# A two-layer encoder trunk on one core: splitting weights further ahead at the start of a feed-forward stage, and a later place for two small steps

## The chip, the cores and the metric

The kernel runs on one core of a Trainium2 chip. The metric is the device time of one execution in microseconds (us). The core has a matrix engine (TensorE, PE in the profile, with its weight loads as PEld), VectorE (DVE), ScalarE (ACT), GpSimd (POOL) and SyncE (SP, which only issues transfers here). Each engine works through its own instructions in order, and semaphores hold an instruction back until its inputs are there.

## The reference

The input x is 256 tokens by 1024, in float32. The network has two layers; each adds half of a gated feed-forward network, then attention of two kinds, then half of a second feed-forward network:

```python
def swiglu(h, w_gate, w_up, w_down):
    return (jax.nn.silu(h @ w_gate) * (h @ w_up)) @ w_down

for l in range(DEPTH):
    x = x + 0.5 * swiglu(rms_norm(x, ffn1_norm[l]), ffn1_w_gate[l], ffn1_w_up[l], ffn1_w_down[l])
    h = rms_norm(x, mix_norm[l])
    proj = h @ w_in[l]
    ...
    x = x + jnp.concatenate([out_a, out_b], axis=-1) @ w_out[l]
    x = x + 0.5 * swiglu(rms_norm(x, ffn2_norm[l]), ffn2_w_gate[l], ffn2_w_up[l], ffn2_w_down[l])
return rms_norm(x, final_norm)
```

The gate and up matrices are 1024 by 2816, the down matrix is 2816 by 1024. So a call runs four feed-forward stages, two per layer.

## The kernel before

**Split products.** TensorE multiplies in a rounded float32 format (`fp32r`). To keep precision every operand is split in two: the high part is the value cast to `fp32r` (by ScalarE), the low part is the value less the high part (by VectorE). A product is then three matmuls: high by high, low by high, high by low. Weights are loaded raw (tiles `raw`, of which there are 6), and split on the core into tiles `w` of the pool `s4` (28 tiles, for everything of that size).

**Steps and the planner.** All weights are listed at the start in the order of use, as steps of 1 MB (`specs`; a step is `Step`, one use of it `Split`). A step is split in two halves, each one cast and one subtraction of 128 x 1024 (`emit_split`, L191 to L217). `ahead(n)` (L228) places, at the point of the program where it is called, the splits of all halves up to number n, the preparations of the steps that need one, and the loads for which a raw tile is free. It is called from `weights` (L249), which hands out the next step i and works ahead up to half 2i + `look[0]` (less an argument), and from `Split.part` (L182), at the first use of the second half of step i, up to half 2i + 1 + `look[0]`; a step taken with `held=True` doesn't make this second call. The number `look[0]` is thus how many halves the splitting runs ahead of the use. All engines but SyncE keep the order in which the program issues their instructions (`Kept`), so where a split is placed decides what it stands behind on ScalarE and on VectorE. SyncE's loads are issued in the order in which they are placed, and each waits until its raw tile has been split.

**A feed-forward stage** (`ffn`, L600) goes through the 2816 columns in five groups of 512 and a rest of 256. Group 0 is plain: four steps (gate and up, for the first and the second half of the 1024 rows) go into the sums `gs` and `us`. While it runs, the norm of the stage is still being finished: the residual's last two turned pairs and the squares (`before(1)`), then the row statistics (`before(2)`, that is `Norm.stats`, L397: mean on VectorE, power -1/2 on GpSimd giving `r`, and half of it, `hr`, on VectorE). `r` is used in the gates (silu, scaled by `r`), `hr` in the up products (`up`, L612). At the end of `before(2)` the accumulating transfers held back till then are issued on GpSimd (`flush`).

**Groups 1 to 4 of a later stage** (`by_seven`, L632) use seven products in place of eight, in the manner of Strassen and Winograd. `SEVEN` names the groups: in the first stage of the call 2, 3 and 4, in the three later ones 1 to 4, so `1 in sevens` is true in these alone. This needs sums of operands:
- of the norm's output: `Norm.copies` (ScalarE) takes float32 copies, `make_sums` (L349) forms four differences on VectorE and splits them; the first two subtractions read only the copies.
- of the weights: raw tiles a, b, c and d. Half of the sums are formed by accumulating transfers on GpSimd (`gather`, L126: b into a, c into b), half by VectorE, which adds c and then d into a (`plus`, L131), two instructions each.

A group has nine steps: a, (b + c), d, c, the first down step, then a three times in its summed forms, and the second down step; in group 1 the order is a, d, down, c, (b + c) and so on. In a group the first product of the gate's upper left part is kept in `m1`, the second added to it on VectorE to give `g0` (for one half of the tokens), and a silu on ScalarE is applied to `g0` in place. `g0` is read only at the end of the group, in `up`.

**look[0]** is 8 in feed-forward stages (`IN_FFN`), but 7 in group 0 of a later one; in groups 1 to 4 of a later stage 8, 7, 6 and 5; 6 (`IN_MIX`) at its end and in attention.

Of the kernel before, what the change touches and what calls it, by code (L numbers as in the profile page):

```python
# [29 lines left out]
IN_FFN, IN_MIX = 8, 6  # L30
# [4 lines left out]
def trunk(ctx: ExitStack, tc: tile.TileContext, x, n1, g1, u1, d1, nm, w_in, sink,  # L35
# [44 lines left out]
    def tmp(tag="tmp", bufs=5, shape=(P, 2, 256), dt=F32):  # L80
        return tp.tile(list(shape), dt, tag=tag, bufs=bufs, name=nm_(tag))
# [143 lines left out]
    look = [IN_MIX]  # L225
# [23 lines left out]
    def weights(less=0, held=False):  # L249

        i = at["use"]
        at["use"] += 1
        if i > 1:
            ahead(2 * i + look[0] - less)
        w = loaded[i]
        w.held = held
        return w
# [48 lines left out]
    class Norm:  # L306
# [90 lines left out]
        def stats(self, n=512):  # L397
            ms = tmp("ms", 2, (P, 2))
            dve.tensor_reduce(ms, self.ss.rearrange("p t (h q) -> p t h q", q=n // 256)[:, :, :, 0],
                              axis=mybir.AxisListType.X, op=ALU.add)  # L400
            dve.tensor_scalar(ms, ms, 1.0 / D, EPS, op0=ALU.mult, op1=ALU.add)
            self.r = tmp("r", 2, (P, 2))
            pool.tensor_tensor(self.r, ms, mhalf[:, 0:2], op=ALU.pow)
            self.hr = tmp("hr", 2, (P, 2))
            dve.tensor_scalar_mul(self.hr, self.r, 0.5)

# [30 lines left out]
    norm = Norm(0)  # L437
# [162 lines left out]
    def ffn(norm, aside=None, before=None, final=False, sevens=SEVEN[1]):  # L600
        def silu(out_, acc, t):
            act.activation(out_, acc, AF.Silu, scale=norm.r[:, t:t + 1])
            return out_

        def gate(gs):
            g = []
            for t in range(2):
                n = gs[t].shape[1]
                g.append(silu(tmp().rearrange("p a n -> p (a n)")[:, :n], gs[t], t))
            return g  # L610

        def up(h, acc, g, t):  # L612
            n = acc.shape[1]
            dve.scalar_tensor_tensor(h[:, t, :n], in0=acc, scalar=norm.hr[:, t:t + 1], in1=g, op0=ALU.mult, op1=ALU.mult)

        def hidden(g, us):
            h = blk(F32)
            for t in range(2):
                up(h, us[t], g[t], t)
            return h  # L620

        def prod(xo, w):
            acc = bank()
            for k in range(4):
                hi, lo = w.part(k)
                xh, xl = xo(k)
                pe.matmul(acc, lhsT=xh, rhs=hi, start=k == 0, stop=False)
                pe.matmul(acc, lhsT=xl, rhs=hi, start=False, stop=False)
                pe.matmul(acc, lhsT=xh, rhs=lo, start=False, stop=k == 3)
            return acc  # L630

        def by_seven(h, g):  # L632


            flat = lambda: tmp().rearrange("p a n -> p (a n)")

            def put(o, x, y, op):
                dve.tensor_tensor(o, x, y, op=op)
                return o

            m1, m7 = flat(), flat()
            if g > 1:
                act.copy(m1, prod(norm.quarter(0, 0), weights()))
                act.copy(m7, prod(norm.summed(3), weights(held=True)))
                hT = turn(h, 2)
                p2 = prod(norm.quarter(0, 1), weights())
                g0 = put(flat(), p2, m1, ALU.add)
                p3 = prod(norm.summed(2), weights())
                silu(g0, g0, 0)
                down(hT, g - 1, 0, weights())  # L650
            else:
                p1 = prod(norm.quarter(0, 0), weights(1, True))
                hT = turn(h, (0,))
                w = weights(1, True)
                act.copy(m1, p1)
                p2 = prod(norm.quarter(0, 1), w)
                hT += turn(h, (1,))
                g0 = put(flat(), p2, m1, ALU.add)
                w = weights()
                silu(g0, g0, 0)  # L660
                down(hT, 0, 0, w)
                p3 = prod(norm.summed(2), weights())
                act.copy(m7, prod(norm.summed(3), weights()))
            h = blk(F32)
            p5 = prod(norm.summed(0), weights())
            late, run = g == max(sevens), 1 in sevens
            p6 = prod(norm.summed(1), weights(look[0] - 5 if late else run, late or run))
            u2 = put(flat(), p6, m1, ALU.subtract)
            u3 = put(m7, m7, u2, ALU.add)
            p4 = prod(norm.quarter(1, 1), weights(look[0] - 4 if late else 3 * run, late or run))  # L670
            g1 = put(m1, p4, u3, ALU.subtract)
            w = weights(look[0] - 3 if late else 2 * run)
            silu(g1, g1, 1)
            put(u3, u3, p5, ALU.subtract)
            put(u2, u2, p5, ALU.subtract)
            put(u2, u2, p3, ALU.add)
            up(h, u2, g0, 0)
            up(h, u3, g1, 1)
            down(hT, g - 1, 1, w)
            return h  # L680

        def turn(hs, n):
            out_ = []
            for i in (range(n) if isinstance(n, int) else n):
                sl = halves(bank())
                for c in range(2):
                    for t in range(2):
                        pe.transpose(sl[:, c, t * P:(t + 1) * P], hs[:, t, (2 * i + c) * P:(2 * i + c + 1) * P], ident)
                hb = blk()
                split(hb, sl)  # L690
                out_.append(hb)
            return out_

        accs = [[bank(), bank()] for _ in range(2)]

        def down(hT, g, h, w):
            tokens(accs[h], [None] * (2 * g) + hT, w, 4 * g, last=(FC - 1, G4 - 1) if final and h else FC - 1)


        gs, us = [bank(), bank()], [bank(), bank()]  # L700
        if before is None:
            before = norm.late
        look[0] = IN_FFN - (1 in sevens)
        before(0)
        ws = (weights(), weights(2))
        for k in (0, 2):
            if k:
                before(1)
            for sl, w in zip((gs, us), ws):
                tokens(sl, norm.xs, w, 0, (k, k + 1))  # L710
                if k and 1 in sevens:
                    norm.copies(2)
        before(2)
        look[0] = IN_FFN
        if 1 in sevens:
            sums = norm.make_sums()
            next(sums)
            w = weights()
            next(sums)
            next(sums)  # L720
            tokens(gs, norm.xs, w, 4)
            w = weights(0, True)
            g = gate(gs)
            next(sums)
        else:
            tokens(gs, norm.xs, weights(), 4)
            g = gate(gs)
            w = weights()
        tokens(us, norm.xs, w, 4)
        h = hidden(g, us)  # L730
        if 1 in sevens:
            next(sums)
        for n in range(1, NGRP):
            if n in sevens:
                look[0] = IN_FFN + min(sevens) - n if before is not take_x else IN_MIX - (n == NGRP - 1)
                h = by_seven(h, n)
                continue
            sums = norm.make_sums()
            gs = [bank(), bank()]
            tokens(gs, norm.xs, weights(), 0)  # L740
            hT = turn(h, 2)
            norm.copies()
            next(sums, None)
            tokens(gs, norm.xs, weights(), 4)
            g = gate(gs)
            next(sums, None)
            us = [bank(), bank()]
            for k0 in (0, 4):
                tokens(us, norm.xs, weights(), k0)
                next(sums, None)  # L750
            h = hidden(g, us)
            for hh in range(2):
                down(hT, n - 1, hh, weights())
                if hh == 0:
                    next(sums, None)

        gu = [bank(), bank()]
        tokens(gu, norm.xs, weights(), 0)
        hT = turn(h, 2)
        tokens(gu, norm.xs, weights(), 4)  # L760
        h = hidden(gate([b[:, 0:256] for b in gu]), [b[:, 256:512] for b in gu])

        def rest():
            hE = turn(h, 1)
            if aside is not None:
                aside()
            return hE
        return accs, hT, rest
# [294 lines left out]
    for l in range(DEPTH):  # L1063
# [7 lines left out]
        if not final:  # L1071
            norm = Norm((l + 1) * 8)
# [76 lines left out]
```

## Time and profile before

| | |
|---|---|
| time, median of 3 runs | 928.06 us (927.64 to 929.15) |
| the profiled execution, its own time | 928.21 us |
| its span | 926.4 us |
| mean granted clock of TensorE | 0.999 |
| ScalarE casts of weights, 128 x 1024 and smaller | 458, mean 952 ns |
| VectorE subtractions of weights | 458, mean 1102 ns |
| VectorE sums of raw tiles | 60, mean 1223 ns |
| HBM read | 199.00 MB, 216 GB/s over the span |

Nearly all instructions carry one line number, that of the helper that issues them (L50), so the profile is read by tiles: `w<-raw` is the cast of a weight half, `w<-raw,w` its subtraction, `raw<-raw,raw` a sum of raw tiles, `tmp<-tmp,r` the silu of a group's g0 or g1, `tmp<-ps,r` a gate of group 0, `ps` anything that TensorE writes. A row of a timeline has the start in us from the span's start, the duration in us (from the first to the last of a merged run), engine, line, operation, output and inputs, shapes, the count behind an x, and in brackets how long the engine had been idle before and what ended that. A row of the waits has engine and output, what it waited for, total us, times, and the longest.

### The profile page before, as it was taken

To read this page: it belongs to the slowest core of one execution; us is meant where nothing else is said; L and a number is where in the kernel's file an instruction comes from. 1 tells how busy PE (TensorE), PEld (TensorE's weight loads), DVE (VectorE), ACT (ScalarE), POOL (GpSimd) and SP (SyncE) were. 2 spreads that over 40 slices of the span, in tenths; PEclk is the share of its full clock that TensorE was granted. 3 is DMA by queue.
4 is the path that set the end of the run, shared out by engine and by line. 5 is a ranking of instruction groups with operands and counts; after the bars stand their busy time and mean duration, and the time that the engine had idled before them with its cause. 6 is when DMAs were issued, how large, how long until landed. Compare 5 with 4: busy or idle time off the path is not lost.

```text
span 926.4 us, 12577 instructions
## 1 busy us (share of the span) xinstructions
PE 909.5 (98%) x4696; PEld 763.2 (82%) x4696; DVE 807.0 (87%) x1125; ACT 590.1 (64%) x917; POOL 65.1 (7%) x83
## 2 busy tenths in 40 slices
PE   8999999999999999999999999999999999999997
PEld 6888887899888888877888887778998888888776
DVE  6769999869875999999779999997698679999994
ACT  7846676567755776576485675665578486675561
POOL 0401000000000100100010010000001010010011
PEclk9999999999999999999999999999999999999999
DMA  9997898837346598897776998787462476998831
GB/s 335 349 236 210 249 268 272 234 104 220 127 139 176 141 291 247 240 265 272 264 170 182 292 261 234 237 289 227 115 230 92 137 170 181 285 273 238 240 134 46
DMA packets 114061, 200.87 MB, mean 217 GB/s; under 512 B 3662, under 2 KB 31376, under 8 KB 114000
## 3 DMA queue, kind: packets, MB, share of 16 engines
q1 hardware_dynamic: 96528, 166.74, 53.6%
q0 software_dynamic: 16096, 31.75, 19.0%
q10 hardware_dynamic: 1376, 1.57, 0.5%
q8 instruction: 37, 0.61, 0.3%
q14 instruction: 24, 0.20, 0.1%
HBM read 199.00 MB, written 1.05 MB: 216 GB/s over the span
## 4 chain that ended last, share of the span: by engine, by line
PE 57%; DVE 26%; DMA 9%; issue 4%; ACT 3%; ACTq 0%; POOLq 0%; DVEq 0%; POOL 0%
PE ps L50 57%; DVE w L50 17%; DMA raw<-in_ffn_w_up_dram 9%; DVE raw L50 3%; DVE tmp L50 3%; ACT w L50 3%; DVE s L50 2%; DMA xk<-in_x_dram 0%; ACT tmp L50 0%; ACTq L50 0%; DVE xk L50 0%; DVEq L50 0%; DVE v L50 0%; POOLq L1144 0%; DVE q L50 0%
## 5 line engine op out<-in xcount | busy, mean ns | idle before, releaser
L50 PE MATMUL ps<-w,s 128*128 128x512 f32 (+1 forms) x2574 | 603.1, 391 | 3.1 <-DVE w L50 3.1
L50 PEld LDWEIGHTS ps<-w,s 128*128 128x128 f32 x2574 | 476.7, 188 | 105.0 <-DVE w L50 6.6
L50 DVE TENSOR_TENSOR w<-raw,w 128x1024 fp32r<-128x1024 f32 (+1 forms) x458 | 482.5, 1102 | 34.8 <-ACT w L50 34.1
L50 ACT CAST w<-raw 128x1024 fp32r<-128x1024 f32 (+1 forms) x458 | 410.8, 952 | 142.8 <-DVE raw L50 96.2
L50 PE MATMUL ps<-w,q 128*128 128x512 f32 x540 | 127.3, 389 | 0.0
L50 PEld LDWEIGHTS ps<-w,q 128*128 128x128 f32 x540 | 101.4, 188 | 21.0
L50 PE MATMUL ps<-s,w 128*128 128x256 f32 x672 | 84.0, 285 | 0.0
L50 PEld LDWEIGHTS ps<-s,w 128*128 128x128 f32 x672 | 81.7, 191 | 1.1
L50 POOL DMA_DIRECT2D raw<-in_ffn_w_up_dram x30 | 38.9, 1295 | 483.6 <-DVE w L50 164.8
L50 DVE TENSOR_TENSOR raw<-raw,raw 128x1024 f32<-128x1024 f32 x60 | 70.7, 1223 | 0.0
L50 ACT ACTIVATE s<-ps,gcol 128x256 fp32r<-128x256 f32 (+1 forms) x80 | 31.7, 480 | 46.9 <-PE ps L50 45.2
L50 PE MATMUL ps<-w,v 128*128 128x512 f32 x180 | 44.1, 391 | 2.9 <-DVE w L50 2.9
L50 PEld LDWEIGHTS ps<-w,v 128*128 128x128 f32 x180 | 33.6, 188 | 11.0 <-DVE w L50 4.2
L50 PE MATMUL ps<-ident,s 128*128 128x128 f32 x304 | 41.2, 274 | 0.2
L50 PEld LDWEIGHTS ps<-ident,s 128*128 128x128 f32 x304 | 35.1, 140 | 6.9 <-DVE s L50 1.2
L50 ACT CAST s<-ps 128x512 fp32r<-128x512 f32 x44 | 24.3, 595 | 23.5 <-PE ps L50 23.5
L50 ACT ACTIVATE s<-s,negm 128x256 f32<-128x256 f32 x64 | 31.9, 500 | 6.6 <-DVE negm L50 6.4
L50 DVE TENSOR_TENSOR tmp<-ps,tmp 128x512 f32<-128x512 f32 x49 | 33.7, 687 | 2.5 <-PE ps L50 1.6
L50 ACT COPY tmp<-ps 128x512 f32<-128x512 f32 x34 | 19.8, 583 | 23.0 <-PE ps L50 17.4
L50 DVE SCALAR_TENSOR_TENSOR s<-ps,gcol,s 128x256 fp32r<-128x256 f32 x48 | 20.3, 478 | 14.9 <-ACT s L50 14.8
L50 DVE TENSOR_TENSOR s<-ps,s 128x512 fp32r<-128x512 f32 x44 | 28.8, 687 | 4.0 <-ACT s L50 4.0
L50 ACT ACTIVATE tmp<-tmp,r 128x512 f32<-128x512 f32 x30 | 21.6, 721 | 15.2 <-DVE tmp L50 15.0
(106 smaller groups left out, 406.8 us busy)
## 6 DMA issues: line engine op xcount, KB each, us to landing
raw<-in_ffn_w_down_dram SPq DMA_DIRECT2D x44, 1024.0 KB, 8.5
raw<-in_ffn_w_gate_dram SPq DMA_DIRECT2D x39, 1024.0 KB, 5.3
raw<-in_ffn_w_up_dram SPq DMA_DIRECT2D x39, 1024.0 KB, 5.2
raw<-in_ffn_w_up_dram POOLq DMA_DIRECT2D x30, 1024.0 KB, 11.5
raw<-in_w_in_dram SPq DMA_DIRECT2D x14, 1024.0 KB, 5.3
raw<-in_ffn_w_gate_dram SPq DMA_DIRECT2D x8, 512.0 KB, 4.6
raw<-in_ffn_w_up_dram SPq DMA_DIRECT2D x8, 512.0 KB, 5.5
raw<-in_w_in_dram SPq DMA_DIRECT2D x8, 512.0 KB, 5.4
```

Of the source, the lines that this page charges most:

```text
L50: ins = issue(*a, **k)
```

## The change

It acts on the three later feed-forward stages (`run = 1 in sevens`), and, in the place of `hr`, on all norms.

1. `look[0]` in group 0: 8 in place of 7 up to the turned pairs, then 9 in place of 7 for the second half of the first two steps, and 9 in place of 8 until group 1, where it is 8 as before.
2. The halving of `r` leaves `stats` and becomes `halve`. It is called behind the sums' first two subtractions in the later stages, and directly behind the statistics in the first one; in the attention stages, which don't use `hr`, it isn't called.
3. The silu of `g0` in groups 1 to 4 of the later stages stands behind the first down product with its splits, not ahead of it.

```diff
@@ Norm.stats
             self.r = tmp("r", 2, (P, 2))
             pool.tensor_tensor(self.r, ms, mhalf[:, 0:2], op=ALU.pow)
+
+        def halve(self):
             self.hr = tmp("hr", 2, (P, 2))
             dve.tensor_scalar_mul(self.hr, self.r, 0.5)
@@ by_seven
+            late, run = g == max(sevens), 1 in sevens
             m1, m7 = flat(), flat()
             if g > 1:
...
                 p3 = prod(norm.summed(2), weights())
-                silu(g0, g0, 0)
+                if not run:
+                    silu(g0, g0, 0)
                 down(hT, g - 1, 0, weights())
+                if run:
+                    silu(g0, g0, 0)
             else:
...
                 g0 = put(flat(), p2, m1, ALU.add)
-                w = weights()
+                down(hT, 0, 0, weights())
                 silu(g0, g0, 0)
-                down(hT, 0, 0, w)
...
-            late, run = g == max(sevens), 1 in sevens
@@ ffn
-        look[0] = IN_FFN - (1 in sevens)
+        look[0] = IN_FFN
         before(0)
         ws = (weights(), weights(2))
         for k in (0, 2):
             if k:
                 before(1)
+                look[0] = IN_FFN + (1 in sevens)
...
         before(2)
-        look[0] = IN_FFN
         if 1 in sevens:
             sums = norm.make_sums()
             next(sums)
+            norm.halve()
             w = weights()
...
         else:
+            norm.halve()
             tokens(gs, norm.xs, weights(), 4)
```

## The prediction

> **What bounds the kernel now.** I read the page's busy shares first, then busy time by windows over one later stage (the feed-forward half that opens layer 1), then the timelines of TensorE, VectorE and ScalarE there.
>
> ```profile
> PE 909.5 (98%) x4696; PEld 763.2 (82%) x4696; DVE 807.0 (87%) x1125; ACT 590.1 (64%) x917; POOL 65.1 (7%) x83
> ...
> PE ps L50 <- DVE w L50: 6.0, 10, 1.0
> ...
> 488.00:607.00 119.00, 117.01 (x529) 95.82 (x528) 117.20 (x121) 75.15 (x87) 7.70 (x6) 1.00 0.84 240
> ```
>
> The windows row is start:end, length, then busy time of TensorE, its weight loads, VectorE, ScalarE and GpSimd. Averaged over the kernel TensorE rules; in the grouped part of a later stage TensorE (117.0 of 119.0) and VectorE (117.2) are level, and the waits row says who is late: in ten places a matmul waits for a low half that VectorE has just written. I take the stalls from starts, since a record (0.39 us) is longer than the pitch of a 512-wide matmul (24 records from 566.99 fill 5.44 us, 0.227 each).
>
> ```profile
> 490.49 0.89 PE L50 MATMUL ps<-ident,s 128*128 128x128 f32 x4
> ...
> 493.96 0.60 PE L50 MATMUL ps<-ident,s 128*128 128x128 f32 x4
> ...
> 566.99 5.61 PE L50 MATMUL ps<-w,q 128*128 128x512 f32 x24
> 572.43 0.63 PE L50 MATMUL ps<-w,s 128*128 128x512 f32 x2
> 573.50 1.67 PE L50 MATMUL ps<-w,s 128*128 128x512 f32 x6 [0.44 <-DVE w L50]
> ...
> 584.07 1.97 PE L50 MATMUL ps<-w,v 128*128 128x512 f32 x8
> 587.01 1.19 PE L50 MATMUL ps<-w,v 128*128 128x512 f32 x4 [0.96 <-DVE w L50]
> ...
> 605.24 0.65 PE L50 MATMUL ps<-w,s 128*128 128x512 f32 x2
> 606.42 1.88 PE L50 MATMUL ps<-w,s 128*128 128x512 f32 x7 [0.52 <-DVE w L50]
> ```
>
> Four losses: the turn at 490.49 takes 0.89 us where the next takes 0.60 (T0 = 0.3); two matmuls from 572.43 should be followed at 572.88 and are at 573.50 (S1 = 0.6); eight from 584.07 at 585.89, but at 587.01 (S2 = 1.1); two from 605.24 at 605.69, but at 606.42 (S3 = 0.7). Together 2.7 us; three later stages of one build hold about 8 us, and that is all the change can win, because nothing else makes TensorE wait there. VectorE runs through without a break from 488 on, so TensorE's end follows VectorE's. To win, VectorE must be ahead when the run begins, or lose its gaps within it.
>
> **Group 0: splits further ahead.** A split of half a step is a ScalarE cast (high half) and a VectorE subtraction (low half). By the planner's counters I number the halves from group 1's first step: h0, h1 (a), h2, h3 (d), h4, h5 (down), h6, h7 (c). Before, h0 comes at gs's second half, h1 and h2 at us's, h3 and h4 behind the sums' subtractions, h5 and h6 around the third step, h7 at group 1. After: h0 before the turned pairs, h1 and h2 at gs's second half, h3 and h4 at us's (before the statistics), h5 behind the subtractions, h6 and h7 with the third and fourth steps. Nothing is added; from group 1 on the order is as before. ScalarE and VectorE in that stretch:
>
> ```profile
> 471.19 1.57 ACT L50 ACTIVATE s<-ps,gcol 128x256 fp32r<-128x256 f32 x4 [3.31 <-PE ps L50]
> ...
> 474.02 1.03 ACT L50 CAST w<-raw 128x1024 fp32r<-128x1024 f32 x1
> 474.96 1.56 ACT L50 ACTIVATE s<-ps,gcol 128x256 f32<-128x256 f32 x4
> ...
> 481.81 1.35 ACT L50 CAST q<-tmp 128x512 fp32r<-128x512 f32 x2
> ...
> 484.96 1.25 ACT L50 ACTIVATE tmp<-ps,r 128x512 f32<-128x512 f32 x2
> ...
> 491.41 0.59 ACT L50 CAST s<-ps 128x512 fp32r<-128x512 f32 x1 [2.62 <-PE ps L50]
> 491.89 2.01 ACT L50 CAST w<-raw 128x1024 fp32r<-128x1024 f32 x2
> ```
> ```profile
> 472.06 1.66 DVE L50 SCALAR_TENSOR_TENSOR s<-ps,gcol,s 128x256 fp32r<-128x256 f32 x4 [1.36 <-ACT s L50]
> 475.09 1.23 DVE L50 TENSOR_TENSOR w<-raw,w 128x1024 fp32r<-128x1024 f32 x1 [1.37 <-ACT w L50]
> 477.49 2.36 DVE L50 TENSOR_TENSOR w<-raw,w 128x1024 fp32r<-128x1024 f32 x2 [1.17 <-ACT w L50]
> ...
> 481.01 0.17 DVE L50 TENSOR_SCALAR hr<-r 128x2 f32<-128x2 f32 x1 [0.89 <-POOL r L50]
> ...
> 489.37 1.41 DVE L50 SCALAR_TENSOR_TENSOR s<-ps,hr,tmp 128x512 f32<-128x512 f32 x2
> ...
> 493.02 0.69 DVE L50 TENSOR_TENSOR s<-ps,s 128x512 fp32r<-128x512 f32 x1
> 493.62 1.22 DVE L50 TENSOR_TENSOR w<-raw,w 128x1024 fp32r<-128x1024 f32 x1
> ```
>
> Prices: casts follow each other at 0.95, subtractions at 1.13, and a subtraction starts 1.07 behind its cast (474.02, 475.09). h0's cast fits into ScalarE's 3.31 us of waiting for TensorE (467.9 to 468.8); its subtraction fills VectorE's gap before 472.06. h1 and h2 are cast from 474.02, four copies follow (1.56), h3 and h4 are cast at 477.5 and 478.4, subtracted until 480.8; the second copies end at 481.0. The statistics come 1.05 us later than before, the sums' first subtraction at 481.1, as before, with two more halves behind it.
>
> **The norm's halving.** `hr` no longer stands ahead of the subtractions, which need only the copies.
>
> ```profile
> 480.27 0.71 POOL L50 TENSOR_TENSOR r<-ms,mhalf 128x2 f32<-128x2 f32 x1 [5.82 <-DVE ms L50]
> 480.95 1.33 POOL L50 DMA_DIRECT2D raw<-in_ffn_w_up_dram  x1
> ...
> 495.08 2.00 ACT L50 CAST w<-raw 128x1024 fp32r<-128x1024 f32 x2
> ...
> 497.09 2.36 DVE L50 TENSOR_TENSOR w<-raw,w 128x1024 fp32r<-128x1024 f32 x2
> ...
> 488.34 0.37 SPq L153 DMA_DIRECT2D raw<-in_ffn_w_gate_dram  x1
> ...
> raw<-in_ffn_w_gate_dram SPq DMA_DIRECT2D x39, 1024.0 KB, 5.3
> raw<-in_ffn_w_up_dram POOLq DMA_DIRECT2D x30, 1024.0 KB, 11.5
> ```
>
> The power ends near 482.0, while VectorE subtracts until 482.5, so the 0.89 us of waiting goes; the halving itself stays (0.1). Its price from both sides: 0.9 saved, or 0.2 if the power and the subtractions get in each other's way for its 0.71 us. Two of the six halvings, in the attention stages, fall away; the diagonals behind them need `r` anyway: nothing. Behind the power on GpSimd waits the transfer that accumulates b into a. It moves from 480.95 to 482.0 and lands, by its median of 11.5 us, at 493.5. Its first reader is the cast at 495.08. The subtraction of that half (497.09) will be 0.9 us earlier, at 496.2 (next paragraph but one), 1.07 behind a cast that may thus still start at 495.1: hidden by 1.6 us. What comes nearer is SyncE's queue. It has one order, and its loads wait for free raw buffers: the load at 488.34 (group 2's first) started when h5 was subtracted, which now happens at 483.8, inside that transfer's time. I take the 1.6 us as enough for one load beside it.
>
> The Trainium skill (SBUF — State Buffer, Who interferes with whom) has a rule against this part: a VectorE instruction with two inputs in SBUF and a GpSimd instruction that reads SBUF shut each other out for a whole instruction. Here the power and the subtractions would come together for the first time, and no row shows such a pair. By the rule the saving is 0.2 and the cushion of the next paragraph is 0.1; the sum would be the same 3.4 us, but only just.
>
> **What of it arrives.** VectorE's work from the first subtraction (481.1) to the gated products (489.37) loses one half of 1.13 and gains the halving: products at 488.4. Ahead of their gates ScalarE has, from 481.0 on, h5's cast, two high halves of the sums (1.35 now, the second after 482.5) and two casts: gates from 485.2 to 486.5, so they hold nothing up. T0 vanishes, and h7 is already done: VectorE is free at 491.0. But next in its order is the low part of the turned block, which waits for TensorE's turn (491.1) and a cast (at 491.1 in place of 491.41): 491.8. So 0.8 us of the lead is lost in a new wait (a cushion for what comes late before it). The cast behind it moves from 491.89 to 491.6, its subtraction from 493.62 to 492.7. **Of two halves (2.3 us) a lead of 0.9 us arrives.**
>
> **Silu behind the down splits.** In group 1, VectorE adds two raw halves and then splits them; the silu stood between the two casts:
>
> ```profile
> 499.36 2.36 DVE L50 TENSOR_TENSOR raw<-raw,raw 128x1024 f32<-128x1024 f32 x2
> ...
> 503.26 1.23 DVE L50 TENSOR_TENSOR w<-raw,w 128x1024 fp32r<-128x1024 f32 x1 [0.34 <-ACT w L50]
> ...
> 501.56 0.72 ACT L50 ACTIVATE tmp<-tmp,r 128x512 f32<-128x512 f32 x1
> ```
>
> Without it the second cast starts when the second sum ends (501.8), its subtraction at 502.87 for 503.26: -0.39. The silu (pitch 0.62) falls where ScalarE waits for the next sums: free. Group 2: -0.39, but two casts later the silu stands ahead of a cast again: 0.95 + 0.95 + 0.62 = 2.52 us of ScalarE against 2 x 1.13 of VectorE, +0.26. Group 4: -0.39, then +0.4 on the half right behind S3, of which 0.3 hides under six matmuls: +0.1 for TensorE. In group 3 it stood nowhere near and now stands behind the last summed half:
>
> ```profile
> 572.22 4.70 DVE L50 TENSOR_TENSOR w<-raw,w 128x1024 fp32r<-128x1024 f32 x4
> ...
> 572.35 4.85 ACT L50 CAST w<-raw 128x1024 fp32r<-128x1024 f32 x5 [0.16 <-DVE raw L50]
> ```
>
> The third subtraction started at 572.22 + 2.26 = 574.48; now not before 572.35 + 0.95 + 0.62 + 1.07 = 574.99: +0.5, behind S1 and ahead of S2.
>
> **Sum.** VectorE's lead is 0.9 + 0.39 + 0.13 = 1.4 at S1, 0.9 at S2, 1.3 at S3. TensorE's own lead is T0 + S1 = 0.9 behind S1, 0.9 behind S2, 1.3 behind S3, less 0.1: **1.2 us** in this stage and in the last one, which has the same rows. In layer 0 one row differs:
>
> ```profile
> 336.20 2.95 ACT L50 CAST w<-raw 128x1024 fp32r<-128x1024 f32 x3 [2.88 <-DMA raw<-in_ffn_w_up_dram]
> ...
> 337.29 3.50 DVE L50 TENSOR_TENSOR w<-raw,w 128x1024 fp32r<-128x1024 f32 x3 [0.33 <-ACT w L50]
> ```
>
> VectorE waits there for an accumulated transfer issued before group 1's silu could gain its 0.39, so that gain is lost: 0.9. Together 3.4 us (1.2 + 1.2 + 0.9, rounded up for the second matmul of each stall, 0.1). The profiled execution took 928.21 us (span 926.4, 1.8 around it), the median is 928.06: 924.8 of the one, **924.7** of the other.
>
> **Rivals.** (A) *Nothing of group 3's 0.5 counts*, since the waits behind it take it up: leads of 1.4 at S2 and 1.8 at S3, 1.7 to 1.8 a stage and 1.4 in layer 0, together 5.0: 923.1. For it: 2.7 us of stall a stage is there to take. Against: VectorE's row at 572.22 is followed by no gap that could take it up.
> (B) *The lead is lost at the turn*: the transfer into a lands 0.7 us too late, or the power does, and 0.2 of the lead is left. TensorE is then 0.2 ahead behind S2 and 0.6 behind S3, less 0.1, and in layer 0 0.1: 1.1 in all, 926.9.
> (C) *Slower: the transfer into a takes the place of the stalls.* After the change two raw buffers are free when SyncE's next two loads are placed (group 0's last and the down step's); if the second down load gets the one that h5 frees, both loads start at 483.8, and the transfer shares its engines with two. At worst it lands a whole median load (5.3) later, 16.8 after its issue, at best of this case half of one, 14.2; between them 15.5: at 497.5, 2.4 us late. The lead is then -1.5; with the silus (0.39 + 0.13 - 0.5 + 0.39 - 0.1 = 0.3) each stage ends 1.2 later: +3.6, 931.6. It decides from 13.1 us between issue and landing and costs over 0.2% from 15. For it: ScalarE waited for such a transfer at 336.20. Against: 14 us lie between its issue (480.95) and the cast now, and no wait is seen.
> (D) *The change does nothing but end T0*: ScalarE's queue eats the lead, and what the silus win group 3 takes back: 0.3 a stage, 927.2.
>
> **How the numbers follow.** Forecast 0.46, A 0.18, B 0.14, C 0.14, D 0.08. The forecast's own range is 923.5 to 926.0. The range of 922.0 to 929.0 leaves out C and a little beyond A. About 0.2% (1.9 us) is what can be told from no change: faster (under 926.2) is the forecast, A and a part of B, 0.70; same the rest of B and D, 0.16; slower C, 0.14.
>
> **What would show it.** Right: `hr` without a wait ahead of it and behind the second subtraction; five subtractions of splits between the pairs and the statistics; a new VectorE wait of 0.8 us for a cast at the turn; no T0; no 0.34 gap in groups 1 and 4; a gap of 0.5 in group 3; S1 gone, S2 hardly smaller. Wrong: ScalarE waiting for the accumulated a at group 1's fifth step (C), or S2 gone too (A).

## The result and the profile after

| | before | after |
|---|---|---|
| median of 10 runs each, same chip | 928.85 us | 925.82 us |
| ratio, 95% interval | | 0.9964 (0.9951 to 0.9978) |
| span of the profiled execution | 926.4 us | 923.2 us |

The changed kernel is 0.36% faster (0.22 to 0.49%), some 3.3 us; the forecast was 3.4 (924.7 us, worked out from a median of 928.06 before, where these ten runs of the kernel before have 928.85). Its page and the waits of TensorE:

```profile
PE 908.6 (98%) x4696; PEld 763.7 (83%) x4696; DVE 807.6 (87%) x1123; ACT 590.6 (64%) x917; POOL 67.7 (7%) x83
```
```profile
PE ps L50 <- DVE w L50: 3.4, 4, 1.3
```

VectorE has two halvings less; otherwise no engine has less to do. What went is waiting: TensorE waits for freshly split low halves in 4 places for 3.4 us, where it was 10 places and 6.0 us. The stage that opens layer 1, TensorE's timeline:

```profile
469.83 1.03 PE L50 MATMUL ps<-ident,xk 128*128 128x128 f32 x8
...
489.77 0.60 PE L50 MATMUL ps<-ident,s 128*128 128x128 f32 x4
...
565.99 5.60 PE L50 MATMUL ps<-w,q 128*128 128x512 f32 x24
571.43 3.79 PE L50 MATMUL ps<-w,s 128*128 128x512 f32 x16
...
582.31 1.98 PE L50 MATMUL ps<-w,v 128*128 128x512 f32 x8
585.18 1.20 PE L50 MATMUL ps<-w,v 128*128 128x512 f32 x4 [0.90 <-DVE w L50]
...
603.45 2.77 PE L50 MATMUL ps<-w,s 128*128 128x512 f32 x9
```

The turn takes 0.60 us, so T0 is gone. The 24 matmuls at 565.99 are followed by 16 in one run: S1 is gone. Eight from 582.31 should be followed at 584.13 and are at 585.18: S2 is still 1.05 us. S3 has no break left in the merged row, but nine matmuls take 2.77 us where 8 pitches of 0.227 and one record of 0.39 make 2.2, so 0.6 us of it is left; the nine took 3.06 before (605.24 to 608.30). VectorE in group 0 and at the turn of group 1, and GpSimd there:

```profile
467.63 3.49 DVE L50 TENSOR_TENSOR w<-raw,w 128x1024 fp32r<-128x1024 f32 x3
471.34 1.66 DVE L50 SCALAR_TENSOR_TENSOR s<-ps,gcol,s 128x256 fp32r<-128x256 f32 x4 [0.22 <-ACT s L50]
474.37 2.36 DVE L50 TENSOR_TENSOR w<-raw,w 128x1024 fp32r<-128x1024 f32 x2 [1.37 <-ACT w L50]
477.72 2.36 DVE L50 TENSOR_TENSOR w<-raw,w 128x1024 fp32r<-128x1024 f32 x2 [0.99 <-ACT w L50]
...
480.26 0.69 DVE L50 TENSOR_TENSOR tmp<-s,s 128x512 f32<-128x512 f32 x1
...
481.59 0.16 DVE L50 TENSOR_SCALAR hr<-r 128x2 f32<-128x2 f32 x1
...
487.47 1.41 DVE L50 SCALAR_TENSOR_TENSOR s<-ps,hr,tmp 128x512 f32<-128x512 f32 x2
...
491.02 0.69 DVE L50 TENSOR_TENSOR s<-ps,s 128x512 fp32r<-128x512 f32 x1 [0.95 <-ACT s L50]
491.97 2.36 DVE L50 TENSOR_TENSOR w<-raw,w 128x1024 fp32r<-128x1024 f32 x2 [0.25 <-ACT w L50]
```
```profile
480.50 1.01 POOL L50 TENSOR_TENSOR r<-ms,mhalf 128x2 f32<-128x2 f32 x1 [6.71 <-DVE ms L50]
481.48 1.33 POOL L50 DMA_DIRECT2D raw<-in_ffn_w_up_dram  x1
```

Five subtractions of splits stand between the pairs and the statistics (the last of the three from 467.63 and the four behind it), `hr` waits for nothing, and a new wait of 0.95 us stands at the turn. To compare runs I count from the turned pairs (470.55 before, 469.83 after): the sums' first subtraction is at 10.5 before and 10.4 after, the products at 18.8 and 17.6, and the first split behind the turned block at 23.1 (493.62) and 22.1. **VectorE is 1.2 us ahead at the products and 0.9 behind the turn.**

The moved silu in group 3, in the timelines of ScalarE and VectorE of the changed kernel:

```profile
571.05 0.72 ACT L50 ACTIVATE tmp<-tmp,r 128x512 f32<-128x512 f32 x1
```
```profile
569.97 2.44 DVE L50 TENSOR_TENSOR w<-raw,w 128x1024 fp32r<-128x1024 f32 x2
572.74 2.36 DVE L50 TENSOR_TENSOR w<-raw,w 128x1024 fp32r<-128x1024 f32 x2 [0.33 <-ACT w L50]
```

It stands between two casts there, and VectorE waits 0.33 us for the second, where it ran through before.

### The profile page after: what moved, and what is told of

The parts are those of the page before. It is cut to its first block, busy times and chain, and to the rows that moved or that the text cites. A ratio compares the mean times of both kernels' runs of the same rounds, so it can differ in the third digit from the quotient of the medians.

```text
span 923.2 us, 12580 instructions
## 1 busy us (share of the span) xinstructions
PE 908.6 (98%) x4696; PEld 763.7 (83%) x4696; DVE 807.6 (87%) x1123; ACT 590.6 (64%) x917; POOL 67.7 (7%) x83
## 3 DMA queue, kind: packets, MB, share of 16 engines
HBM read 199.00 MB, written 1.05 MB: 217 GB/s over the span
## 4 chain that ended last, share of the span: by engine, by line
PE 85%; DVE 11%; issue 2%; DMA 1%; ACT 1%; SPq 0%; POOLq 0%; POOL 0%; DVEq 0%; ACTq 0%
PE ps L50 85%; DVE w L50 7%; DVE raw L50 2%; DVE tmp L50 1%; DVE s L50 1%; DMA raw<-in_ffn_w_gate_dram 1%; ACT w L50 1%; ACT tmp L50 0%; SPq L156 0%; DVE xk L50 0%; POOLq L1150 0%; POOL rf L50 0%; SPq L422 0%; DVEq L50 0%; ACTq L50 0%
```

## The experiments

**How they are compared.** The profiled executions differ in the first stage, which no edit here concerns except for the place of one halving and the absence of another: from the span's start to the turned pairs of layer 0's second feed-forward stage (TensorE's row at 291.75 in the kernel before, 291.74 after) it takes up to 3 us more in some, also for the same kernel (294.01 in a second profile of the changed one). So beside the ratio I give the time from this **mark** to the end of TensorE's work (920.08 before, 916.81 after): 628.3 before, 625.1 after. Each such time is that of one profiled execution; the two of the changed kernel differ by 0.4 us: by 0.5 in layer 0's stage, and by under 0.1 in each of layer 1. Where it matters I also give the time by stage, from turned pairs to turned pairs: layer 0, the first of layer 1, and the last to the end (178.8, 277.1 and 172.4 before; 178.1, 275.8 and 171.2 after; 177.6, 275.8 and 171.3 in the second profile of the change).

| kernel | ratio to before, 95% | span | mark to end | S2 in layer 1, first stage |
|---|---|---|---|---|
| before | | 926.4 | 628.3 | 1.12 |
| the change | 0.9964 (0.9951 to 0.9978) | 923.2 | 625.1 | 1.06 |
| the change again | 0.9966 (0.9957 to 0.9976) | 925.0 | 624.7 | 1.12 |
| splits ahead alone | 0.9970 (0.9958 to 0.9982) | 923.8 | 625.7 | 1.11 |
| silus alone | 0.9990 (0.9981 to 1.0000) | 925.5 | 627.3 | 1.50 |
| halving alone | 0.9964 (0.9950 to 0.9978) | 923.6 | 625.1 | 1.12 |
| splits ahead and halving | 0.9977 (0.9966 to 0.9988) | 925.3 | 625.2 | 1.13 |
| the change, group 3's silu back | 0.9955 (0.9940 to 0.9971) | 922.5 | 623.4 | 0.59 |
| the change, silus late | 0.9946 (0.9932 to 0.9959) | 921.2 | 623.2 | 0.74 |
| the change, first turn covered | 0.9955 (0.9942 to 0.9969) | 921.9 | 623.9 | 0.87 |
| silus late, both turns covered | 0.9935 (0.9923 to 0.9948) | 921.9 | 620.9 | 0 |
| silus late, halving, no splits ahead | 0.9936 (0.9915 to 0.9956) | 920.4 | 622.3 | 0.56 |
| the same, both turns covered | 0.9942 (0.9919 to 0.9965) | 920.4 | 622.5 | 0.52 |

S2 is the start of the ninth of the twelve matmuls (`w,v`) in group 4, less the start of the eighth and one pitch.

**The parts alone.** Theory: whatever VectorE wins in group 0, at the turn it must wait for TensorE's transposes and ScalarE's cast, so that the lead behind the turn has a cap. Rival: the parts add. The splits alone:

```diff
-        look[0] = IN_FFN - (1 in sevens)
+        look[0] = IN_FFN
...
                 before(1)
+                look[0] = IN_FFN + (1 in sevens)
...
         before(2)
-        look[0] = IN_FFN
```

> Only group 0's splits stand further ahead; the halving and the silu are as before. Theory (the turn of group 1 caps the lead: whatever is won before it, VectorE must wait there for TensorE's turn and ScalarE's cast): VectorE again waits 0.9 to 1.0 us for the power, now 1 us later, its gated products start near 0.1 us before the present, but h7 is already done and the low part of the turned block starts 1.1 us earlier, so the lead behind the turn is 0.8 to 0.9 us; S1 and S3 shrink by that, S2 stays near 1.1: span 2.3 to 2.7 us below the kernel before. Rival (the parts simply add): the halving brings its 0.9 us a stage, so without it and the silus only 0.3 us a stage is left: span 0.5 to 1.0 us below.

The halving alone (`halve` called behind `next(sums)`, or behind the statistics in the first stage, and not in attention; nothing else):

> Only the halving stands behind the first two subtractions (and is gone in attention). Theory (capped at the turn): VectorE's 0.9 us wait for the power goes, the power takes about 1.0 us beside the subtractions, products start 0.8 us earlier, T0 goes, the turned block's low part starts 0.8 us earlier behind h7, hardly any wait at the turn: lead 0.8 us, and the span 2.1 to 2.5 us below the kernel before, nearly as much as the splits ahead alone would bring, because the two do the same work on one cap. Rival (parts add): the halving brings what the whole change brings less the other two parts, with the splits ahead the larger: 1 us below or less.

The silus alone (the hunks in `by_seven`):

> Only the silu of g0 moves behind the first down product. Theory: VectorE wins 0.39 and 0.13 in groups 1 and 2, loses 0.33 to 0.5 in group 3, wins 0.39 in group 4 and loses 0.3 right behind: T0 stays, S1 shrinks by 0.4 to 0.5, S2 grows by as much, S3 shrinks by 0.4: span 0.6 us below the kernel before (0.2 to 1.0). Rival (the silus are what made the change fast): span 2 us below or more.

VectorE around the turn, with TensorE's turned pairs in the second fence of each; the splits alone:

```profile
490.88 0.69 DVE L50 TENSOR_TENSOR s<-ps,s 128x512 fp32r<-128x512 f32 x1
491.83 2.36 DVE L50 TENSOR_TENSOR w<-raw,w 128x1024 fp32r<-128x1024 f32 x2 [0.26 <-ACT w L50]
```
```profile
469.59 1.03 PE L50 MATMUL ps<-ident,xk 128*128 128x128 f32 x8
```

The halving alone:

```profile
490.04 1.22 DVE L50 TENSOR_TENSOR w<-raw,w 128x1024 fp32r<-128x1024 f32 x1
491.17 0.68 DVE L50 TENSOR_TENSOR s<-ps,s 128x512 fp32r<-128x512 f32 x1
491.83 2.36 DVE L50 TENSOR_TENSOR w<-raw,w 128x1024 fp32r<-128x1024 f32 x2
```
```profile
469.69 1.03 PE L50 MATMUL ps<-ident,xk 128*128 128x128 f32 x8
```

The first split behind the turn comes 22.2 and 22.1 us behind the pairs, as with the whole change (22.1; 23.1 before). Either part alone fills the same 0.9 us. The halving alone makes 3.2 us from the mark, as much as the whole change makes (3.3 and 3.6 in its two profiles); by the span it is 2.8, above the 2.1 to 2.5 expected. The splits alone make 2.7 (by the span 2.6, as expected), but S3 stays at 0.7 where the expectation had it shrink; it stays with the halving alone too. The silus alone make 1.0 (0.6, 0.4 and nothing by stage), more than the 0.6 expected and within its bounds (TensorE's timeline of that kernel):

```profile
571.87 11.30 PE L50 MATMUL ps<-w,s 128*128 128x512 f32 x48
583.01 1.98 PE L50 MATMUL ps<-w,v 128*128 128x512 f32 x8
586.33 1.20 PE L50 MATMUL ps<-w,v 128*128 128x512 f32 x4 [1.34 <-DVE w L50]
```

By pitches the 48 matmuls should take 11.06 us, so 0.24 is left of S1, which by the same sum was 0.74 before; S3, by this sum, falls from 0.86 to 0.56, and S2 grows by the 0.4 that group 3 takes.

**Two parts together.** The change with the silus as before:

```diff
-                if not run:
-                    silu(g0, g0, 0)
+                silu(g0, g0, 0)
                 down(hT, g - 1, 0, weights())
-                if run:
-                    silu(g0, g0, 0)
...
-                down(hT, 0, 0, weights())
+                w = weights()
                 silu(g0, g0, 0)
+                down(hT, 0, 0, w)
```

> The changed kernel with the silus back where they were: the splits further ahead and the halving together. Each alone brought the span from 926.4 to 923.8 and to 923.6. Theory (one cap at the turn): together no more than the better of them and what T0 leaves: 923.2 to 923.8, with a VectorE wait of about 0.95 us at the turn that neither has alone. Rival (they add): 926.4 - 2.6 - 2.8 = 921.0.

VectorE at the turn of this kernel, then its turned pairs on TensorE:

```profile
492.54 0.69 DVE L50 TENSOR_TENSOR s<-ps,s 128x512 fp32r<-128x512 f32 x1 [0.97 <-ACT s L50]
493.49 2.36 DVE L50 TENSOR_TENSOR w<-raw,w 128x1024 fp32r<-128x1024 f32 x2 [0.26 <-ACT w L50]
```
```profile
471.32 1.04 PE L50 MATMUL ps<-ident,xk 128*128 128x128 f32 x8
```

The span is 925.3, outside the 923.2 to 923.8 expected, but 2.0 us of it are in the first stage; from the mark it is 625.2, and the first split behind the turn is again 22.2 behind the pairs. The wait at the turn (0.97) is the work that the two parts do twice over: had they added, 2.7 and 3.2 would have left 622.4. Here the rival falls, and it falls in every stage: the halving alone gains 1.3, 1.0 and 1.0 us, the splits alone 1.0, 0.9 and 0.8, both together 1.3, 1.0 and 1.0.

What the silus bring once the other parts are there follows from this kernel and the whole change. In the two stages of layer 1 the change is faster by 0.4 and 0.3 us in its first profile, by 0.3 and 0.2 in its second; in layer 0's it is 0.5 slower in the first and equal in the second. Over the whole that is 0.1 or 0.5 us, too little to be told.

**The silu in group 3.** Its old place there, the new one in the others (`if not run or g == 3`, and the reverse below):

> The changed kernel with the silu of group 3 alone back at its old place; groups 1, 2 and 4 as changed. Theory (the new 0.34 us gap in group 3 comes straight off the lead at S2): the gap goes, S2 and what follows end 0.25 to 0.34 us earlier in each later stage: span 0.7 to 1.0 below the changed kernel, 922.2 to 922.5. Rival (a wait behind it takes the gap up anyway): within 0.2 of 923.2.

The ratio's interval overlaps the change's, but from the mark it is 1.7 us faster than the change (1.3 than the change again), more than the 0.7 to 1.0 expected, and S2 falls by half (TensorE's timeline of this kernel):

```profile
582.60 1.98 PE L50 MATMUL ps<-w,v 128*128 128x512 f32 x8
585.01 1.21 PE L50 MATMUL ps<-w,v 128*128 128x512 f32 x4 [0.43 <-DVE w L50]
```

So the gap in group 3 does come straight off S2. In each stage of layer 1 the kernel gains 0.5 us, where the gap was 0.33; where the rest comes from stays open.

**The silu late.** Directly ahead of the silu of `g1`, in all four groups:

```diff
-                if run:
-                    silu(g0, g0, 0)
...
-                silu(g0, g0, 0)
...
+            if run:
+                silu(g0, g0, 0)
             silu(g1, g1, 1)
```

> The changed kernel with the silu of g0 in the later stages' groups moved further, directly ahead of that of g1, where the next casts are not needed for some microseconds. Theory: the gaps of 0.15, 0.34 and 0.33 us in groups 2, 3 and 4 all go and none comes: 0.5 us more lead at S2 than the changed kernel, S3 gone: span 1.2 to 1.8 below it, 921.4 to 922.0. Rival (the silu ahead of the group's last sums delays the up products, or the next group's casts): a gap of 0.3 us or more ahead of the products, span 923 or more.

From the mark 1.9 us below the change (expected 1.2 to 1.8), the span 921.2. The gaps of groups 2 to 4 are gone; S3, expected to go, is still 0.4. In layer 0 one wait stays, and it is not the silu's (ScalarE's timeline of this kernel, then VectorE's):

```profile
335.31 2.95 ACT L50 CAST w<-raw 128x1024 fp32r<-128x1024 f32 x3 [3.36 <-DMA raw<-in_ffn_w_up_dram]
```
```profile
336.39 3.50 DVE L50 TENSOR_TENSOR w<-raw,w 128x1024 fp32r<-128x1024 f32 x3 [0.80 <-ACT w L50]
```

**The turns covered.** First the first turn alone, on the changed kernel:

```diff
-                p1 = prod(norm.quarter(0, 0), weights(1, True))
+                p1 = prod(norm.quarter(0, 0), weights(0, True))
```

> The changed kernel with one argument more changed: in group 1 of the later stages the first step's use works ahead one half further, so that the first half of b + c is split ahead of the turn. Theory (the lead is lost in VectorE's 0.95 us wait at the turn): that wait is filled with this subtraction (1.13), the lead behind the turn grows by 0.8 to 0.9 us a stage, S2 falls from 1.0 to 1.6 to near 0.3, S3 goes: span 2.0 to 2.7 us below the changed kernel (920.5 to 921.2). Rival (S2 is set by a transfer or by TensorE and not by VectorE's lead): S2 stays, span within 0.5 us of the changed kernel.

VectorE at the two turned blocks of this kernel:

```profile
490.06 0.68 DVE L50 TENSOR_TENSOR s<-ps,s 128x512 fp32r<-128x512 f32 x1
...
493.16 0.69 DVE L50 TENSOR_TENSOR s<-ps,s 128x512 fp32r<-128x512 f32 x1 [1.02 <-ACT s L50]
```

The wait of 0.95 us is gone from the first turned block and stands at the second: 1.02. So 1.2 us came from the mark, not 2.0 to 2.7, since the second block is a cap too, which the expectation had not seen. And of the 1.2 only 0.2 and 0.1 lie in the stages of layer 1; 0.9 lie in layer 0 (0.5 against the second profile of the change), where VectorE waited 0.81 us (0.39 in the second) for an accumulated transfer, and waits for none here. Covering the first turn alone is thus worth next to nothing. Then both (the same edit to the second `weights(1, True)`), with the late silu:

> The late silu, and in group 1 both turns covered: the first two steps work ahead one half further, so the half behind each turn is split ahead of it. The first alone moved VectorE's wait from the first turned block (0.95) to the second (1.02), and brought 1.3 us. Theory (the lead is whatever isn't waited away at the turns): the wait at the second turn is filled too, unless the accumulated a has not landed when its cast comes (10 us from its issue); the lead grows by another 0.8 to 1.0 a stage, S2 falls under 0.4: span 919.0 to 920.5. Rival (the accumulated a is late): ScalarE waits for the transfer in front of the turned block's cast, TensorE waits for the block, span 921 or more.

TensorE at the place of S2 in this kernel, then VectorE in group 1:

```profile
583.22 3.02 PE L50 MATMUL ps<-w,v 128*128 128x512 f32 x12
```
```profile
513.61 0.69 DVE L50 TENSOR_TENSOR tmp<-ps,tmp 128x512 f32<-128x512 f32 x1 [0.87 <-PE ps L50]
```

Twelve matmuls in one run: S2 is gone in this stage, and in group 1 VectorE now waits 0.87 us for TensorE, so there the engines have changed places. From the mark it is 620.9, 4.2 us below the change and 2.3 below the late silu alone; of these 2.3, 0.7 and 0.3 lie in layer 1, and 1.3 in layer 0, where the wait of 0.80 for the accumulated transfer is gone. The span expected (919.0 to 920.5) was missed; the first stage took 2.9 us more in this execution. The runs have a median of 921.36.

**Are the splits ahead worth anything?** The late silu and the moved halving, with `look[0]` in group 0 as before, without and with the turns covered:

> The late silu and the moved halving, with the splits of group 0 as before the change. Time is read from the last layer-0 attention transposes (291.75 us in the kernel before) to the end of TensorE's work, since the runs' first stage differs by up to 3 us: 628.3 before, 625.1 with the change, 623.2 with the late silu. Theory (the turn caps the lead, so the splits ahead are worth nothing once the halving is moved): 623.0 to 623.6, as with them. Rival (the splits ahead bring a part of it): 624.0 or more.

> The best kernel (late silu, both turns covered) with the splits of group 0 as before the change. From the same mark to the end it has 620.9. Theory (with the turns covered the cap is gone, and only then do the splits ahead count): VectorE reaches the first turned block later by what it no longer has in hand, 0.9 to 1.1 us a stage, and S2 comes back in part: 622.5 to 623.8. Rival (the splits ahead never count): 621.2 or less.

Without the cover the splits ahead are worth nothing: 622.3 without them (623.0 to 623.6 expected), 623.2 with them. 0.7 of the 0.9 us lie in layer 0, where VectorE does not wait for the accumulated transfer as it does in the late-silu kernel (0.80). VectorE's timeline in layer 0 of the kernel without the splits and without the cover:

```profile
335.86 3.50 DVE L50 TENSOR_TENSOR w<-raw,w 128x1024 fp32r<-128x1024 f32 x3
```

With both turns covered it is 622.5 without them and 620.9 with them. By stages the 1.7 us are 1.0, 0.6 and 0.1. The 0.6 is S2, which comes back in the first stage of layer 1 (0.52) and is gone with the splits ahead. In layer 0 the kernel without them waits for the accumulated transfer (VectorE's timeline), which the kernel with them does not:

```profile
336.01 3.50 DVE L50 TENSOR_TENSOR w<-raw,w 128x1024 fp32r<-128x1024 f32 x3 [0.59 <-ACT w L50]
```

So the splits ahead count under the cover in one stage for certain; how much of layer 0's 1.0 is theirs is open, and the last stage shows next to nothing. The times of whole runs (0.9935 and 0.9942, their intervals overlapping) can't tell the two kernels apart. Without the splits the cover brings nothing over 622.3; in layer 1 the two kernels agree to 0.1 us, as VectorE has nothing in hand to fill the turns with.

> The changed kernel once more, on the chip of these runs, as their measure: 625.1 from the mark to the end within 0.2, the whole 0.3 to 0.4% below the kernel before.

It came out at 624.7, 0.4 below the first profile and outside the 0.2 given. In layer 0 the wait for the accumulated transfer was 0.39 us this time and 0.81 the first; from issue to landing that transfer took 12.9 and 13.6 us. Over all the kernels here without a covered turn it took 12.7 to 13.6, so layer 0 alone can move by half a microsecond, and differences under 0.5 us that lie there are not read.

## Why the prediction was right

**Time and steps.** From the mark the gain is 3.3 us in the first profile of the change and 3.6 in the second. By stages it is 0.7, 1.3 and 1.2 in the first and 1.2, 1.3 and 1.2 in the second, where 0.9, 1.2 and 1.2 were forecast. The mechanism held; that the sum fits to 0.1 us is partly luck, as two executions of one kernel differ by more.

- Statistics 1.05 later: they are 0.95 later (counted from the pairs). First subtraction where it was: yes.
- Lead 0.9 behind the turn with a new wait of 0.8: 0.9 and 0.95. This was the step that decided the size, and it held in every run that has both the splits ahead and the halving and no turn covered.
- T0 and S1 gone, S2 hardly smaller: as forecast. S2 in layer 0 even grew, from 1.1 to 1.5 and 1.4.
- Gap in group 3 of 0.5: 0.33. Group 4: the gap ahead of S3 went and one of 0.33 stands behind it, as worked out.
- The accumulated transfer into a hides behind its cushion: ScalarE waits for it in no run. The prediction let it take 11.5 us and land 1.6 ahead of its first cast; it took 8.2 before and takes 10.1 now (491.59), 2.5 ahead of the cast (494.08). So it did become slower, as rival C feared, but stayed below the 13.1 us from which C decides.
- Rival A falls with S2, which is still there and halves when group 3's silu goes back; B falls with the lead of 0.9, D with S1.
- "VectorE runs through without a break from 488 on" was too strong: its own row at 503.26 has a gap of 0.34, and there are three more of 0.16 to 0.34 in that stage. The silus were moved to close such gaps.

**What it had too simple.** The prediction wrote the 0.9 us under the splits: "of two halves a lead of 0.9 us arrives". It had priced the halving at 0.9 us saved, and then let it end in the cushion of the turn, without asking what the halving would do if the splits were not there. The runs answer it: the halving alone brings 3.2 us, the splits alone 2.7, both together 3.2. The sum was right because it was cut off at the turn, not because the larger part was the one that worked.

**The silus** were put at 0.3 us in each stage of layer 1 and at nothing in layer 0. In layer 1 they brought 0.2 to 0.4 a stage, as the change shows against the kernel with the two other parts. For layer 0 the prediction reasoned that the accumulated transfer comes at its own time, so that group 1's 0.39 only turns into a longer wait for it, 0.33 + 0.39 = 0.72. The first profile of the changed kernel seems to bear that out (VectorE's timeline, layer 0):

```profile
336.47 3.50 DVE L50 TENSOR_TENSOR w<-raw,w 128x1024 fp32r<-128x1024 f32 x3 [0.81 <-ACT w L50]
```

But in the second profile the wait is 0.39, and with the silus alone it is 0.15. From issue to landing the transfer took 13.6, 12.9 and 12.9 us in these three (13.3 before), so the wait follows the transfer's time as much as the silu. And the halving alone gained 1.3 us in layer 0, where 0.9 was forecast for the whole change; its transfer took 12.9 us. What the silu does there is therefore not shown.

**A rule that held on one side.** For the halving the Trainium skill (SBUF — State Buffer, Who interferes with whom) was weighed: two-input VectorE instructions and a GpSimd instruction that reads SBUF shut each other out. The power, 0.70 to 0.73 us wherever it runs by itself, took 1.08, 1.01 and 1.01 beside the subtractions, which kept their 0.69. In all thirty cases (ten profiles with the moved halving) it ended 0.56 to 0.58 us behind the end of the first subtraction (480.95 and 481.51 in the rows above), 0.30 us longer where 0.44 of that subtraction was left at its start and 0.37 where 0.51 was. That fits a power held up until the subtraction under way has ended, on GpSimd's side as the rule has it. The other direction, which the prediction's price of 0.2 rests on, is not seen: the second subtraction starts 0.04 us behind the first, as before, and `hr` waits for nothing.

## What to carry to other kernels

A lead won on an engine is worth what gets past the next place where that engine must wait for another in its own order; find that place before adding up the parts, since everything ahead of it shares one cap, and the cheapest part that reaches the cap (here one small instruction moved past a wait) is enough. To win more, put work that needs nobody ahead of every such wait: with one turn covered the wait only moved on to the next; with both covered the splits ahead began to count (0.6 us in the stage where it can be read), and with the late silu this gave the fastest kernel from the mark. A small instruction between two casts costs only where the other engine is waiting for the second one, so look for a stretch where nobody is.

## What was not expected of the hardware

The power on GpSimd was lengthened by half (0.71 to between 1.01 and 1.08 us) beside VectorE's subtractions, by an amount that grew with what was left of the first of them, while these kept their time. An accumulating transfer of 1 MB at one and the same place took 12.9 us in one execution of the changed kernel and 13.6 in another. And the first third of that kernel took 2.3 us more in the one than in the other (mark at 294.01 and 291.74), so one span alone would have ranked several of these kernels wrongly; why it varies was not tried.
